# Regions at multiples of 512 bytes, and a planner that issues in a second pass

## The chip, the cores and the metric

One core of a Trainium2 chip runs the whole program in one launch. The metric is the device time of one execution in microseconds; it is compared as the median of several executions, and each text names the run it speaks of. Engines are named as in the profile: PE (TensorE, the matrix unit; PEld are its weight loads), DVE (VectorE), ACT (ScalarE), POOL (GpSimd) and SP (SyncE, which here issues all DMAs).

## The reference

The kernel computes a decoder trunk of two layers over 256 positions with a width of 1024, in float32. Each layer has a feed-forward part, a mixer and a second feed-forward part; a norm ends it:

```python
for l in range(DEPTH):
    x = x + FFN_HALF * swiglu(rms_norm(x, ffn1_norm[l]), ffn1_w_gate_up[l], ffn1_w_down[l])
    u = rms_norm(x, mix_norm[l]) @ w_in[l]
    u_ssd, u_ml, u_rw = jnp.split(u, [D_SSD_IN, D_SSD_IN + D_MLSTM_IN], axis=-1)
    y_ssd = ssd_mixer(u_ssd, ...)      # Mamba-2: convolution, decays, two chunks of 128
    y_ml = mlstm_mixer(u_ml, ...)      # chunked matrix memory with gates
    y_rw = rwkv7_mixer(u_rw, ...)      # a recurrence over time, 8 heads of 64
    y = jnp.concatenate([y_ssd, y_ml, y_rw], axis=-1)
    x = x + y @ w_out[l]
    x = x + FFN_HALF * swiglu(rms_norm(x, ffn2_norm[l]), ffn2_w_gate_up[l], ffn2_w_down[l])
return rms_norm(x, final_norm)
```

The weights are some 200 MB and are read once; the activations are small.

## The kernel before

**The work.** Activations stay on the chip. Each piece of weights (128 x 1024 floats, 512 KB) comes by DMA into a raw buffer. ACT (L784) and DVE (L785) split it into a high and a low half in the PE's fast float format, and three matmuls (L817, L818, L819: high-high, high-low, low-high) make up one product at nearly full precision. In the feed-forward parts L1036, L1038 and L1041 do the like with the activations as the moving side. The mixer's own small products are in plain float32; one such instruction shows as two records of the profile.

**The mixer.** Its combined projection is done in blocks of 128 columns (24 matmuls of 256 columns each, L817 to L819), in a fixed order of groups. A block is evacuated by ACT (L1156, L1155) and DVE (three L1158, a causal convolution) or the like. Meanwhile the three mixers run as soon as their columns are there. In the RWKV part, DVE inverts small triangular blocks in a chain of short instructions (L1327, L1329, L1331), SP writes the result and its transpose to DRAM (`dg`, L1334; `dh`, L1335) and reads them back in another layout (L1343, 16 small DMAs). PE transposes other operands in the meantime (L1351, evacuated by ACT L1353; L1363, whose bank DVE L1366 and ACT L1364 and L1365 read). Then five sets of 64x64 products (L1393, 32 instructions each) complete the inverse, with ACT (L1402, L1411) and DVE (L1406, L1407, L1413) between them; the first needs dg, the second dh. L1439, L1444, L1450, L1453 and L1435 are the recurrence over the four chunks. L1577 and L1578 (evacuated by L1581) make decays; L1599, L1608, L1628, L1654 are the mLSTM; L1720 (transposes, read by DVE L1721 and L1723), L1739 (DVE) and L1751 (PE) are the SSD; L1170 are transposes of finished outputs, which go into the product with `w_out`.

**Buffers.** Nearly all data lie in 22 regions of 2048 floats per partition, each cut into 16 blocks of 128 floats. A region is either of kind `f` (float32) or `r` (the fast format) and may change its kind when it is empty. Behind the constants and one tile `smalls` the regions follow one another in memory, 8192 bytes each.

**What sets the order.** All engine calls are first recorded as operations. A planner, `Planner.run`, then goes through them like a list scheduler: it keeps a model time for each engine, looks at each engine's available operations, takes the one that can start first (by its class and rank among equals), gives its new buffers a place and issues it. `find` looks for the place: raw weights (class `w`) go to the high end of a hole, all else to the low end; the hole that is free soonest and is smallest wins. `may_open` and `keep_max` hold space back. So the queue of every engine is what the planner made of costs and free space, and where a buffer lies decides what can be placed next to it, and when. In this version each operation is issued at the moment it is planned.

Of the kernel before, what the change touches and what calls it, by code (L numbers as in the profile page):

```python
# [64 lines left out]
class Buf:  # L65


    def __init__(self, kind, n, cls):
        self.kind, self.n, self.cls, self.group = kind, n, cls, None
        self.left, self.place, self.where, self.end = 0, None, None, 0.0  # L70
        self.acc = []
        self.pe = None
        self.dests = []
# [79 lines left out]
class Op:  # L153
    __slots__ = ("line", "n", "eng", "call", "name", "a", "k", "bufs", "left", "succ", "ready", "cross", "occ", "dur", "table", "tail",
                 "rank", "piece", "dense", "gate", "lock", "issued", "nbytes", "start", "wait_all")


class Planner:
# [18 lines left out]


    def turn(self, i, kind):
        self.sides[i] = kind  # L180
        self.tiles[i] = self.pool.tile([128, BLOCKS * GRAIN], F32 if kind == "f" else F32R, tag=f"region{i}",
                                       name=f"region{i}")

    def new(self, n, cls="t", kind="f"):
        buf = Buf(kind, n, cls)
        if cls == "t" and kind == "f" and self.group:
            buf.group = self.group
            self.wanted[self.group] = self.wanted.get(self.group, 0) + n
        v = self.tiles[0][:, 0:n]
        return Ref(buf, v if kind == "f" else v.bitcast(F32R))  # L190
# [21 lines left out]
    def add(self, eng, name, call, a, k):  # L212
# [28 lines left out]
        op.left = len(preds)  # L241
# [15 lines left out]
    def touch(self, op, v, write, preds):  # L257
        if isinstance(v, Ref):
            if v.buf not in op.bufs:
                op.bufs.append(v.buf)  # L260
                v.buf.left += 1
            acc = v.buf.acc
            if v.buf.kind == "bank" and op.eng == "pe":

                if v.buf.pe is not None:
                    preds.add(v.buf.pe)
                v.buf.pe = op
        elif v.space == "DRAM" or "dram" in v.tensor.name:
            w = self.dram.setdefault(v.tensor.name, [])
            if write:  # L270
                w.append(op)
            else:
                preds.update(w)
            return
        else:
            acc = self.base.setdefault(v.tensor.name, [])
# [81 lines left out]
    def run(self, reserve, wmin, wmax, urgent, keep_max, spare):  # L358
        ops = self.ops
        for op in reversed(ops):  # L360
            op.tail = op.dur + max((s.tail for s in op.succ), default=0.0)
# [13 lines left out]
        def find(buf, t):  # L375
# [10 lines left out]
            if buf.group:  # L386

                keep = min(keep_max, sum(self.wanted.get((buf.group[0], g), 0) for g in range(buf.group[1])))
# [7 lines left out]
            for i in range(REGIONS):  # L396
                empty = st["free"][i] == BLOCKS
                if st["free"][i] < n or (self.sides[i] != buf.kind or self.tiles[i] is None) and not empty:
                    continue
# [4 lines left out]
                if empty and (self.sides[i] != buf.kind or n == BLOCKS):  # L404
# [18 lines left out]
        def may_open(buf):  # L423

            left = sum(1 for i in range(REGIONS) if st["free"][i] == BLOCKS or self.sides[i] == "r")
            return left > (spare if buf.cls == "w" and st["w"]["f"] >= wmin["f"] else wmin["r"])

        def taken(buf, i):
            buf.where = i
            if buf.kind == "bank":  # L430
                bank_free[i] = INF
                used[buf.cls] += 1
                buf.place = self.banks[i]
            elif buf.kind == "small":
                slot_free[i] = INF
                buf.place = self.smalls[:, i * SLOT:i * SLOT + buf.n]
            else:
                (i, j), n = i, -(-buf.n // GRAIN)
                if self.sides[i] != buf.kind or self.tiles[i] is None:
                    self.turn(i, buf.kind)  # L440
# [4 lines left out]
                buf.place = self.tiles[i][:, j * GRAIN:j * GRAIN + buf.n]  # L445
                if buf.cls == "w":
                    st["w"][buf.kind] += 1
                if buf.group:
                    self.wanted[buf.group] -= buf.n
# [66 lines left out]
        while todo:  # L516
# [18 lines left out]
            assert best is not None, self.stuck(avail, used, grid, st)  # L535
# [3 lines left out]
            for b in places(op):  # L539
# [4 lines left out]
                taken(b, i)  # L544
            if op.lock:
                start = max(start, t)
            if op.table and op.table != st["table"]:
                st["table"] = op.table
                self.nc.scalar.preload_act_table_set(
                    "natural_log_exp_and_others" if op.table == "E" else "silu_and_others")  # L550
# [31 lines left out]
            todo -= 1  # L582

# [7 lines left out]
def kernel(ctx: ExitStack, tc: tile.TileContext, x, pvec, prow, fnorm, w_gate,  # L591
# [27 lines left out]
    smalls = const.tile([128, SLOT * SLOTS], F32, name="smalls")  # L619
# [1308 lines left out]
```

## Time and profile before

| | |
|---|---|
| median of the 3 runs | 1295.01 us (1294.98 to 1297.09) |
| the profiled execution | 1296.8 us |
| its span, first to last instruction | 1294.9 us |
| PE, DVE, ACT, POOL busy | 97%, 69%, 55%, 7% of the span |
| DMA | 210.22 MB, 162 GB/s in the mean |
| mean granted clock of PE | 0.993 |

Times in the profile's rows count from the start of the span. The first feed-forward part lasts to about 199 us, the mixer of layer 0 to about 459, two feed-forward parts to about 840, the mixer of layer 1 to about 1096, the last feed-forward part to the end. A row of idle time names what ended it; PE's ends are modelled, so idle time of PE is a lower bound of what it lost.

### The profile page before, as it was taken

Reading aid. Unit: us, or ns where it says so; the run is one execution under the profiler, and the core shown is the slowest. Engines: PE = TensorE matmul, PEld = TensorE weight load, DVE = VectorE, ACT = ScalarE, POOL = GpSimd, SP = SyncE. Lnnn points to the kernel's source line nnn. Section 1 sums busy time; section 2 is a strip of 40 time slices with the busy share of each in tenths; the row PEclk is TensorE's granted clock in tenths of the full one; section 3 lists DMA queues with packets and bytes.
Section 4 is the critical chain, followed back from the end, with each engine's and each line's share of the span. In section 5 each row is a group of like instructions: output and inputs, shape, how many; then the busy total and the mean of one; then the engine's idle time right before and its main releaser. Section 6 shows DMA issues by size and latency. Waiting matters only on the chain.

```text
span 1294.9 us, 20867 instructions
## 1 busy us (share of the span) xinstructions
PE 1249.7 (97%) x7890; PEld 1077.5 (83%) x7890; DVE 894.7 (69%) x1442; ACT 715.1 (55%) x1241; POOL 90.1 (7%) x161
## 2 busy tenths in 40 slices
PE   7999999987999999999999999999899999999997
PEld 6888887986997878888878888779789888888886
DVE  6766666984699566666676666669837984766664
ACT  7555545664654365555465555565556543655553
POOL 3000002120100010000000000011201010000001
PEclk9999999998999999999999999999999999999999
DMA  9996645152065967765576666530513575976300
GB/s 288 320 292 184 189 129 131 34 124 49 18 220 203 265 185 215 221 187 150 175 217 187 186 193 179 147 82 3 139 34 115 180 257 165 280 208 189 121 1 33
DMA packets 281876, 210.22 MB, mean 162 GB/s; under 512 B 23856, under 2 KB 257200, under 8 KB 281776
## 3 DMA queue, kind: packets, MB, share of 16 engines
q1 hardware_dynamic: 281776, 208.89, 55.4%
q8 instruction: 62, 1.02, 0.3%
q14 instruction: 38, 0.31, 0.1%
HBM read 207.01 MB, written 1.84 MB: 161 GB/s over the span
## 4 chain that ended last, share of the span: by engine, by line
PE 85%; DVE 6%; ACT 3%; DMA 2%; SPq 1%; issue 1%; POOL 0%; POOLq 0%; DVEq 0%; ACTq 0%
PE bank L1036 20%; PE bank L819 13%; PE bank L818 13%; PE bank L817 13%; PE bank L1038 12%; PE bank L1041 3%; PE bank L1393 1%; DVE region L785 1%; PE bank L1751 1%; DMA region<-in_f_gu_dram 1%; DMA region<-dn 1%; ACT region L784 1%; PE bank L1444 1%; PE bank L1453 1%; PE bank L1608 1%
## 5 line engine op out<-in xcount | busy, mean ns | idle before, releaser
L785 DVE TENSOR_TENSOR region<-region,region 128x1024 fp32r<-128x1024 f32 (+1 forms) x382 | 444.4, 1208 | 57.1 <-ACT region L784 52.5
L1036 PE MATMUL bank<-region,region 128*128 128x512 f32 x1120 | 398.2, 398 | 0.0
L817 PE MATMUL bank<-region,region 128*128 128x512 f32 (+1 forms) x1104 | 386.7, 350 | 0.5 <-DVE region L1267 0.4
L818 PE MATMUL bank<-region,region 128*128 128x512 f32 (+1 forms) x1104 | 384.7, 349 | 0.0
L819 PE MATMUL bank<-region,region 128*128 128x512 f32 (+1 forms) x1104 | 384.1, 349 | 0.5 <-DVE region L836 0.5
L784 ACT ACTIVATE region<-region 128x1024 fp32r<-128x1024 f32 (+1 forms) x382 | 376.1, 1038 | 7.6 <-DVE region L1676 2.1
L1038 PE MATMUL bank<-region,region 128*128 128x256 f32 x1280 | 346.5, 281 | 0.0
L1036 PEld LDWEIGHTS bank<-region,region 128*128 128x128 f32 x1120 | 210.4, 188 | 50.9
L1038 PEld LDWEIGHTS bank<-region,region 128*128 128x128 f32 x1280 | 241.6, 189 | 6.5
L819 PEld LDWEIGHTS bank<-region,region 128*128 128x128 f32 x1104 | 210.1, 190 | 27.9 <-DVE region L836 1.5
L818 PEld LDWEIGHTS bank<-region,region 128*128 128x128 f32 x1104 | 210.0, 190 | 25.9 <-issue 0.5
L817 PEld LDWEIGHTS bank<-region,region 128*128 128x128 f32 x1104 | 210.1, 190 | 25.7 <-issue 1.3
L1049 ACT ACTIVATE region<-bank 128x256 f32<-128x256 f32 (+1 forms) x84 | 30.9, 373 | 220.2 <-PE bank L1041 220.2
L1051 DVE TENSOR_TENSOR region<-bank,region 128x256 f32<-128x256 f32 (+1 forms) x84 | 34.2, 410 | 127.0 <-ACT region L1049 127.0
L836 DVE TENSOR_TENSOR region<-region,region 128x256 fp32r<-128x256 f32 (+2 forms) x88 | 36.9, 424 | 35.6 <-ACT region L835 35.6
L1053 ACT ACTIVATE region<-region 128x256 f32<-128x256 f32 (+1 forms) x84 | 34.0, 408 | 49.3 <-DVE region L1052 49.3
L1041 PE MATMUL bank<-region,region 128*128 128x512 f32 x160 | 60.2, 399 | 0.0
L835 ACT ACTIVATE region<-region 128x256 fp32r<-128x256 f32 (+2 forms) x88 | 36.2, 416 | 37.4 <-DVE region L1055 37.0
L853 POOL TENSOR_SCALAR smalls<-smalls 128x1 f32<-128x1 f32 x14 | 6.7, 479 | 616.3 <-ACT region L849 616.0
L849 ACT ACTIVATE region<-res 128x512 f32<-128x512 f32 x28 | 17.6, 629 | 54.0 <-DVE res L845 51.5
L1158 DVE SCALAR_TENSOR_TENSOR region<-bank,pv,region 128x255 f32<-128x255 f32 (+2 forms) x84 | 39.6, 479 | 5.9 <-ACT region L1155 2.9
L1055 DVE TENSOR_TENSOR region<-region 128x256 f32<-128x256 f32 (+1 forms) x76 | 32.0, 422 | 10.9 <-ACT region L1053 2.4
(310 smaller groups left out, 1086.4 us busy)
## 6 DMA issues: line engine op xcount, KB each, us to landing
region<-in_f_gu_dram SPq DMA_DIRECT2D x352, 256.0 KB, 5.4
region<-in_f_dn_dram SPq DMA_DIRECT2D x88, 512.0 KB, 4.8
region<-in_w_in_dram SPq DMA_DIRECT2D x80, 512.0 KB, 4.8
region<-in_w_out_dram SPq DMA_DIRECT2D x32, 512.0 KB, 4.9
region<-in_prow_dram SPq DMA_DIRECT2D x4, 512.0 KB, 5.2
region<-in_prow_dram SPq DMA_DIRECT2D x6, 256.0 KB, 3.7
region<-in_w_gate_dram SPq DMA_DIRECT2D x2, 512.0 KB, 3.6
dn<-region SPq DMA_DIRECT2D x64, 4.0 KB, 1.5
```

The source lines that it names most:

```text
L784: act.activation(out=hi[:, c], in_=src[:, c], func=AF.Copy)
L785: dve.tensor_tensor(out=lo[:, c], in0=src[:, c], in1=hi[:, c].bitcast(F32), op=ALU.subtract)
L817: pe.matmul(o, lhsT=ah, rhs=bh, start=start, stop=False, skip_group_check=True)
L818: pe.matmul(o, lhsT=ah, rhs=bl, start=False, stop=False, skip_group_check=True)
L819: pe.matmul(o, lhsT=al, rhs=bh, start=False, stop=stop, skip_group_check=True)
L835: act.activation(out=hi, in_=src, func=AF.Copy)
L836: dve.tensor_tensor(out=lo, in0=src, in1=hi.bitcast(F32), op=ALU.subtract)
L1036: pe.matmul(o, lhsT=wh[:, k, g, :], rhs=hT.both(kk), start=kk == 0, stop=False, skip_group_check=True)
L1038: pe.matmul(o[:, T:], lhsT=wl[:, k, g, :], rhs=hT(kk)[0], start=False, stop=False, skip_group_check=True)
L1041: pe.matmul(o, lhsT=wh[:, k, g, :], rhs=hT.both(kk), start=False, stop=True, skip_group_check=True)
L1051: dve.tensor_tensor(out=s[:, ts], in0=gate[:, ts], in1=s[:, ts], op=ALU.add)
L1158: dve.scalar_tensor_tensor(out=dst[:, s:T], in0=ps[:, 0:T - s], scalar=col(cw + 3 - s), in1=dst[:, s:T], op0=ALU.mult, op1=ALU.add)
```

## The change

Three things change in the source. The tile `smalls` gets 56 more columns (224 bytes), so region 0 starts at byte 40960 of a partition instead of 40736: 0 instead of 288 past a multiple of 512 bytes, and all regions with it. The planner no longer issues while it plans: `run` only notes for each operation its place in the order, the buffers that it opens and the regions that change their kind, and `emit` issues them afterwards; with that, `run` can be tried with several `keep_max` until one yields a plan. And the list of kinds is kept differently: a region not yet used was of kind `f` before, and has no kind now, except region 0.

```diff
-        self.sides, self.tiles = ["f"] * REGIONS, [None] * REGIONS
+        self.tiles = [None] * REGIONS
         self.turn(0, "f")
+        self.template = self.tiles[0]
...
     def run(self, reserve, wmin, wmax, urgent, keep_max, spare):
+
         ops = self.ops
+        bufs = {b for op in ops for b in op.bufs}
+        for b in bufs:
+            b.left, b.place, b.where, b.end = b.uses, None, None, 0.0
+        wanted = dict(self.wanted)
+        for op in ops:
+            op.left, op.issued, op.ready, op.cross, op.start, op.turns, op.placed = op.npred, False, 0.0, 0.0, None, [], []
+        sides = ["f"] + [None] * (REGIONS - 1)
...
-                if st["free"][i] < n or (self.sides[i] != buf.kind or self.tiles[i] is None) and not empty:
+                if st["free"][i] < n or sides[i] != buf.kind and not empty:
                     continue
...
-                if empty and (self.sides[i] != buf.kind or n == BLOCKS):
+                if empty and (sides[i] != buf.kind or n == BLOCKS):
                     fits.append((max(float(blocks.max()), t), BLOCKS, i, 0))
                     continue
...
-                buf.place = self.tiles[i][:, j * GRAIN:j * GRAIN + buf.n]
+                buf.place = True
...
-            assert best is not None, self.stuck(avail, used, grid, st)
+            if best is None:
+                self.jam = self.stuck(avail, used, grid, st)
+                return False
...
-            call_from(op.line, op.call, [v.at() if isinstance(v, Ref) else v for v in op.a],
-                      {n: v.at() if isinstance(v, Ref) else v for n, v in op.k.items()})
-            op.issued = True
+            op.issued = len(log)
...
+    def emit(self):
+
+        for op in sorted(self.ops, key=lambda op: op.issued):
...
+            for b in op.placed:
...
+                    b.place = self.tiles[i[0]][:, i[1] * GRAIN:i[1] * GRAIN + b.n]
+            call_from(op.line, op.call, [v.at() if isinstance(v, Ref) else v for v in op.a],
+                      {n: v.at() if isinstance(v, Ref) else v for n, v in op.k.items()})
...
-    smalls = const.tile([128, SLOT * SLOTS], F32, name="smalls")
+    smalls = const.tile([128, SLOT * SLOTS + 56], F32, name="smalls")
...
+    assert any(plan.run(reserve={"f": 6144, "r": 6144}, wmin={"f": 4, "r": 4}, wmax={"f": 5, "r": 6},
+                        urgent={"act": 7000.0, "dve": 5500.0}, keep_max=keep, spare=8)
+               for keep in (3072, 4096, 6144, 8192)), plan.jam
     with tc.manual_schedule():
-        plan.run(reserve={"f": 6144, "r": 6144}, wmin={"f": 4, "r": 4}, wmax={"f": 5, "r": 6}, urgent={"act": 7000.0, "dve": 5500.0}, keep_max=3072, spare=8)
+        plan.emit()
```

The last of the three changes `find`: an `f` buffer that opens an unused region now falls under `sides[i] != buf.kind` and is put at block 0, where a raw weight was put at the region's high end before. From there on free space lies otherwise, and the plan differs from some point on. The lines of the mixer stand 30 lines further down in the new source (L1363 is L1393 there, L1393 is L1423, L817 is L847).

The engines get the same instructions in the same numbers. PE's order is the same up to the second group of L1363 in layer 0. Before, at the place where PE waits for dg and dh, its queue has the rest of a block (weights in `region_2317`), transposes, and then the 64x64 products (L1393):

```order
L817 MATMUL bank_88<-region_628,region_2317 128x256
L818 MATMUL bank_88<-region_628,region_2317 128x256
L819 MATMUL bank_88<-region_628,region_2317 128x256
L1351 MATMUL bank_90<-ident,region_1811 128x128 x4
L1351 MATMUL bank_91<-ident,region_1811 128x128 x4
L1439 MATMUL bank_89<-region_2520,region_2178 64x64 x4
L1439 MATMUL bank_89<-region_2520,region_347 64x64 x4
L1351 MATMUL bank_88<-ident,region_1811 128x128 x4
L1363 MATMUL bank_90<-ident,region_1859 128x128 x4
L1351 MATMUL bank_91<-ident,region_1811 128x128 x4
L1393 MATMUL bank_88<-region_827,region_584 64x64 x4
```

Now PE takes the second L1363 (L1393 in the new source) at once and goes on with a new block (weights in `region_672`):

```order
L848 MATMUL bank_88<-region_175,region_2319 128x256
L849 MATMUL bank_88<-region_175,region_2319 128x256
L1393 MATMUL bank_90<-ident,region_1860 128x128 x4
L847 MATMUL bank_91<-region_628,region_672 128x256
L848 MATMUL bank_91<-region_628,region_672 128x256
L849 MATMUL bank_91<-region_628,region_672 128x256
```

and the first 64x64 products (now L1423) come behind the last matmul of that block, two of the next, a group of transposes and a first L1599 (now L1629):

```order
L849 MATMUL bank_91<-region_175,region_672 128x256
L847 MATMUL bank_89<-region_628,region_2061 128x256
L848 MATMUL bank_89<-region_628,region_2061 128x256
L1381 MATMUL bank_90<-ident,region_911 128x128 x4
L1629 MATMUL bank_92<-region_696,region_1841 128x128
L1423 MATMUL bank_93<-region_846,region_1704 64x64 x4
```

In all, 26 projection matmuls moved ahead of the first 64x64 product, and 15 between these products. On ACT, which evacuates the banks at the same place, the order before is:

```order
L1365 ACTIVATE region_2623<-bank_89 64x512
L1353 ACTIVATE region_942<-bank_90 128x512
L1353 ACTIVATE region_892<-bank_91 128x512
L1581 ACTIVATE region_2520<-bank_92,region_892 128x128
L1441 ACTIVATE region_2674<-bank_89 64x512
L1353 ACTIVATE region_2674<-bank_88 128x512
L1364 ACTIVATE region_2623<-bank_90 64x512
```

and now (L1364 is L1394, L1365 is L1395, L1581 is L1611, L1441 is L1471, L1353 is L1383, L1156 is L1186, L1402 is L1432):

```order
L1395 ACTIVATE region_2625<-bank_89 64x512
L1394 ACTIVATE region_2625<-bank_90 64x512
L1395 ACTIVATE region_1040<-bank_90 64x512
L1611 ACTIVATE region_2522<-bank_92,region_1841 128x128
L1611 ACTIVATE region_2522<-bank_93,region_1841 128x128
L1611 ACTIVATE region_2522<-bank_87,region_1841 128x128
L1471 ACTIVATE region_1841<-bank_88 64x512
L1383 ACTIVATE region_2665<-bank_89 128x512
```

The second L1364 and L1365 moved ahead of the evacuations of L1351. SP's queue there is the same: dg, dh, eight and eight DMAs back.

More of the change, by code (lines that the diff above doesn't have):

```diff
@@ L69, in __init__ @@
         self.kind, self.n, self.cls, self.group = kind, n, cls, None
-        self.left, self.place, self.where, self.end = 0, None, None, 0.0
+        self.left, self.place, self.where, self.end, self.uses = 0, None, None, 0.0, 0
         self.acc = []
@@ L154 @@
     __slots__ = ("line", "n", "eng", "call", "name", "a", "k", "bufs", "left", "succ", "ready", "cross", "occ", "dur", "table", "tail",
-                 "rank", "piece", "dense", "gate", "lock", "issued", "nbytes", "start", "wait_all")
+                 "rank", "piece", "dense", "gate", "lock", "issued", "nbytes", "start", "wait_all", "npred", "turns", "placed")
 class Planner:
@@ L188, in new @@
             self.wanted[self.group] = self.wanted.get(self.group, 0) + n
-        v = self.tiles[0][:, 0:n]
+        v = self.template[:, 0:n]
         return Ref(buf, v if kind == "f" else v.bitcast(F32R))
@@ L240, in add @@
                 v.buf.dests += [b for b in op.bufs if b.kind in "fr" and b not in v.buf.dests]
-        op.left = len(preds)
+        op.npred = len(preds)
         for p in preds:
@@ L260, in touch @@
                 op.bufs.append(v.buf)
-                v.buf.left += 1
+                v.buf.uses += 1
             acc = v.buf.acc
@@ L386, in find @@
             if buf.group:
-                keep = min(keep_max, sum(self.wanted.get((buf.group[0], g), 0) for g in range(buf.group[1])))
+                keep = min(keep_max, sum(wanted.get((buf.group[0], g), 0) for g in range(buf.group[1])))
                 if (st["room"] - n) * GRAIN < keep:
@@ L423, in may_open, with taken @@
         def may_open(buf):
-            left = sum(1 for i in range(REGIONS) if st["free"][i] == BLOCKS or self.sides[i] == "r")
+            left = sum(1 for i in range(REGIONS) if st["free"][i] == BLOCKS or sides[i] == "r")
             return left > (spare if buf.cls == "w" and st["w"]["f"] >= wmin["f"] else wmin["r"])
-        def taken(buf, i):
+        def taken(op, buf, i):
             buf.where = i
+            op.placed.append(buf)
             if buf.kind == "bank":
@@ L432, in taken @@
                 used[buf.cls] += 1
-                buf.place = self.banks[i]
+                buf.place = True
             elif buf.kind == "small":
                 slot_free[i] = INF
-                buf.place = self.smalls[:, i * SLOT:i * SLOT + buf.n]
+                buf.place = True
             else:
                 (i, j), n = i, -(-buf.n // GRAIN)
-                if self.sides[i] != buf.kind or self.tiles[i] is None:
-                    self.turn(i, buf.kind)
+                if sides[i] != buf.kind:
+                    sides[i] = buf.kind
+                    op.turns.append((i, buf.kind))
                 grid[i, j:j + n] = INF
@@ L444, in taken @@
                 st["ver"] += 1
-                buf.place = self.tiles[i][:, j * GRAIN:j * GRAIN + buf.n]
+                buf.place = True
                 if buf.cls == "w":
@@ L448, in taken @@
                 if buf.group:
-                    self.wanted[buf.group] -= buf.n
+                    wanted[buf.group] -= buf.n
         def released(buf):
@@ L582, in run @@
             todo -= 1
+        return True
+    def emit(self):
+        for op in sorted(self.ops, key=lambda op: op.issued):
+            for turn in op.turns:
+                if isinstance(turn, str):
+                    self.nc.scalar.preload_act_table_set(
+                        "natural_log_exp_and_others" if turn == "E" else "silu_and_others")
+                else:
+                    self.turn(*turn)
+            for b in op.placed:
+                i = b.where
+                if b.kind == "bank":
+                    b.place = self.banks[i]
+                elif b.kind == "small":
+                    b.place = self.smalls[:, i * SLOT:i * SLOT + b.n]
+                else:
+                    b.place = self.tiles[i[0]][:, i[1] * GRAIN:i[1] * GRAIN + b.n]
+            call_from(op.line, op.call, [v.at() if isinstance(v, Ref) else v for v in op.a],
+                      {n: v.at() if isinstance(v, Ref) else v for n, v in op.k.items()})
     def stuck(self, avail, used, grid, st):
```

6 lines of the change are left out of this document (2 added, 4 removed).

## The prediction

> **What bounds the kernel now.** I read four views, from the whole to the place: the page, the waits of TensorE, the timeline around the longest of them, and the stretches behind it.
>
> ```profile
> span 1294.9 us, 20867 instructions
> PE 1249.7 (97%) x7890; PEld 1077.5 (83%) x7890; DVE 894.7 (69%) x1442; ACT 715.1 (55%) x1241; POOL 90.1 (7%) x161
> PE 85%; DVE 6%; ACT 3%; DMA 2%; SPq 1%; issue 1%; POOL 0%; POOLq 0%; DVEq 0%; ACTq 0%
> q1 hardware_dynamic: 281776, 208.89, 55.4%
> ```
>
> TensorE is busy for 1249.7 of 1294.9 us, so whatever is done to the rest can win at most the 45.2 us in which it stands still. DMA is 2% of the chain that ended last. The waits of TensorE over the whole run (us in total, times, longest) say where those 45 us lie:
>
> ```profile
> PE bank L1363 <- DVE region L1567: 8.6, 2, 6.6
> PE bank L885 <- DMA res<-in_x_dram: 6.2, 2, 4.3
> PE bank L1393 <- DMA region<-dh: 2.2, 1, 2.2
> PE bank L1393 <- DMA region<-dg: 1.2, 1, 1.2
> ```
>
> The first, third and fourth row belong to one place in the mixer of layer 0. There DVE has solved small triangular systems, SP sends the result through DRAM (dg, dh) and back, and the 64x64 products of L1393 wait for it. The timeline there, first TensorE, then SP, DVE and ACT (start, length, in brackets the idle time before and what ended it):
>
> ```profile
> 287.11 0.28 PE L818 MATMUL bank<-region,region 128*128 128x256 f32 x1
> ...
> 289.27 0.28 PE L818 MATMUL bank<-region,region 128*128 128x256 f32 x1
> 296.17 1.08 PE L1363 MATMUL bank<-ident,region 128*128 128x128 f32 x4 [6.63 <-DVE region L1567]
> ...
> 300.04 1.17 PE L1439 MATMUL bank<-region,region 128*64 128x64 f32 x16 [0.22 <-issue]
> ...
> 303.83 2.38 PE L1393 MATMUL bank<-region,region 64*64 64x64 f32 x64 [1.15 <-DMA region<-dg]
> 308.41 6.01 PE L1393 MATMUL bank<-region,region 64*64 64x64 f32 x192 [2.20 <-DMA region<-dh]
> 314.81 2.08 PE L1393 MATMUL bank<-region,region 64*64 64x64 f32 x64 [0.39 <-ACT region L1411]
> 316.82 1.56 PE L1608 MATMUL bank<-region,region 128*128 128x256 f32 x6
> 321.99 0.61 PE L1599 MATMUL bank<-region,region 128*128 128x128 f32 x4
> 322.43 1.06 PE L1450 MATMUL bank<-region,region 128*128 128x128 f32 x8
> ```
>
> ```profile
> 296.96 3.85 SPq L1343 DMA_DIRECT2D region<-dg  x8
> 300.91 5.26 SPq L1343 DMA_DIRECT2D region<-dh  x8
> ...
> 302.35 0.69 DVE L1366 TENSOR_TENSOR region<-bank,smalls 128x512 f32<-128x512 f32 x1 [1.47 <-PE bank L1351]
> ...
> 303.07 0.59 ACT L1364 ACTIVATE region<-bank 64x512 f32<-64x512 f32 x1 [0.52 <-DVE region L1366]
> ```
>
> So behind the 6.63 us come four more stops: 0.22 + 1.15 + 2.20 + 0.39 = 3.96 us. In all of them TensorE has projection work that it could do but that stands later in its queue. Behind this place the changed stretch of layer 0, and all of the changed stretch of layer 1, have none:
>
> ```profile
> 323.70:356.10 32.40, 32.40 (x322) 30.71 (x321) 19.70 (x45) 21.82 (x46) 5.22 (x6) 1.00 0.06 18
> 356.10:388.50 32.40, 32.40 (x266) 30.91 (x267) 30.19 (x51) 19.10 (x28) 2.67 (x2) 1.00 0.69 220
> 388.50:420.80 32.30, 32.30 (x166) 24.95 (x165) 29.72 (x38) 15.20 (x25) 2.87 (x4) 1.00 0.56 203
> 1003.50:1035.90 32.40, 32.40 (x203) 28.03 (x203) 31.20 (x46) 18.44 (x25) 2.75 (x2) 1.00 0.55 180
> ```
>
> (Columns: stretch, its length, then busy us and instructions of PE, PEld, DVE, ACT, POOL, the granted clock, the DMA share and GB/s.) TensorE fills each stretch; DVE comes close to it in three of the four.
>
> **The change, part by part.** It says that it moves addresses. The order says that it also moves instructions, so there are three parts.
>
> *Addresses.* The pad puts the regions from 288 bytes past a multiple of 512 to 0. If an engine cared, tiles that lie elsewhere would read or write at another pace already: `res` lies 384 past, `br` and `selr` 160 and 128 past.
>
> ```profile
> L849 ACT ACTIVATE region<-res 128x512 f32<-128x512 f32 x28 | 17.6, 629 | 54.0 <-DVE res L845 51.5 <-DMA res<-in_x_dram 2.1
> L1767 ACT ACTIVATE region<-region 128x512 f32<-128x512 f32 x8 | 5.0, 626 | 15.1 <-DVE region L1766 15.1
> L845 DVE SCALAR_TENSOR_TENSOR res<-bank,smalls,res 128x512 f32<-128x512 f32 x16 | 11.4, 745 | 8.3 <-PE bank L819 7.5 <-POOL region L951 0.9
> L1770 DVE SCALAR_TENSOR_TENSOR region<-region,smalls,region 128x512 f32<-128x512 f32 x8 | 5.6, 744 | 0.6 <-POOL smalls L831 0.6
> L1577 PEld LDWEIGHTS bank<-br,selr 128*128 128x128 f32 x40 | 6.0, 189 | 0.2
> L1038 PEld LDWEIGHTS bank<-region,region 128*128 128x128 f32 x1280 | 241.6, 189 | 6.5
> ```
>
> 629 against 626, 745 against 744, 189 against 189 ns: I cost the addresses at 0 for ACT, DVE and TensorE. No tile here lies at 0 past 512, so a gain at exactly that place is not excluded; the rows nearest to it say none. For the transfers nothing in the trace separates the old address from another one. The bound comes from who waits: TensorE's three DMA rows above are 6.2 + 2.2 + 1.2 = 9.6 us, of which the 6.2 us are for `res`, which does not move. A transfer would have to become a fifth shorter to show even 2 us. I take 0, with bounds from -2 us (a fifth of 9.6) to +2 us.
>
> The Trainium skill, "DMA: Bandwidth & Descriptors", section "How a descriptor splits into AXI transactions", says that a descriptor which does not start at a multiple of 256 bytes fetches from the boundary below it, and pays for the bytes ahead of its start. It tells this of reads, and here the regions are mostly written; for a run of 512 bytes that starts 32 past the boundary it would be 17 beats of 32 bytes instead of 16, by my estimate from that page 6%. The sum would then be lower by 6% of 9.6 us, 0.6 us. No row here shows it.
>
> *Two passes.* The plan is made first and issued afterwards; the instructions that TensorE, DVE, ACT, POOL and SP get are the same in number and kind (the built orders differ in place alone), and the first of the four values of `keep_max`, the old 3072, already yields a plan. What it costs on the chip: 0, since planning is done before there is a program.
>
> *The order.* Because unopened regions now count as neither kind, the first raw weights go to the low end of their region and the free space falls otherwise. From the second group of transposes of L1363 on, the plan of layer 0 differs, that of layer 1 from 991 us of the old run on (the first L1170 that stands elsewhere). Ahead of that, and with it the wait of 6.63 us and all of the start, nothing is moved. At the place above 41 matmuls of the projections (L817 to L819, 256 columns) come ahead: 15 + 1 + 10 behind the second L1363 and before the first L1393, 1 + 14 between the L1393; so do the eight matmuls of L1599. Their prices: from 287.11 to 289.27 are 18 matmuls, so 0.12 us each, 41 x 0.12 = 4.9 us; L1599 takes (322.43 - 321.99) / 4 = 0.11 us a record and makes two records an instruction, 16 x 0.11 = 1.8 us. Together 6.7 us of work, more than the 3.96 us of holes. SP's row of dg and dh transfers stands where it stood, so dh still lands at about 308.4.
>
> I follow the new queue of TensorE with those rows. It has the second L1363 at about 298.8, the 15 matmuls until 301.3 (the clock is half until about 300, as before), L1439 until 302.4, the transposes L1351 with 11 matmuls between them until 305.9. The dg products thus start two us later than at 303.83, when dg has long landed: the 0.22 and 1.15 are gone. ACT is what is late next. It now has L1364 directly behind L1365, and this waits for DVE's second L1366, which stands behind three instructions of L1158, until about 301.6, and ACT idles for some 1.6 us in which it evacuated L1351 before; so the bank that the second half of the dg products needs is read out at about 306.6, 0.4 us after TensorE wants it. The dg products end at 308.7, when dh is there: the 2.20 us is gone. The rest of L1599 follows (until 310.3), the next 96 products (6.0 us, until 316.4), 14 matmuls (1.7 us, which cover L1411 and its 0.39 us) and the last 32 (2.1 us): 320.2 us, where the old kernel stands at 316.8. It is 3.4 us later there with 6.7 us more done. Gain 3.3 to 3.4 us; I take 3.4.
>
> *What lies behind.* The 41 matmuls are missing as cover later. In layer 0, between the transposes L1720 and the products L1751 there are now 10 projection matmuls instead of 14, and DVE's work on them must be done meanwhile. DVE is the tight engine there (29.72 and 30.19 of 32.4). It is helped by the same move, since splits of weights (L785) that stood there now stand ahead of 335 us, where it idles. I cost it at 0, cover being what is left of the projections; the bounds are 0 and the rival below. In layer 1 nothing waits in the changed part, so nothing can be won and I take 0 there too, bounds 0 and +2 us (a wait as long as dh's above).
>
> **The sum.** -3.4 us on the profiled execution's 1296.8 us (span 1294.9 and 1.9 around it) gives 1293.4. That execution lies 1.8 us above the median of the runs, 1295.01, so I forecast the median at 1291.6. About 0.2%, 2.6 us, is what a measurement of this kernel can tell from no change.
>
> **Rivals.**
> - *Given back.* The place gains as worked out, but one or two small waits of the size of dg's and dh's rows (1.2 to 2.2 us) appear behind it, in layer 0 where DVE is tight or in layer 1. For it: DVE at 92% and 96% of two stretches. Against: the old plan had the same load there and no wait of TensorE. Time: 1291.6 + 1.2 to 1291.6 + 3.4, about 1294.
> - *DVE becomes the bound in layer 0's tail (slower).* Place: the first L1751 behind L1720. There DVE has in a row three L1739, an L1723, an L1730, a fourth L1739 and a split L785. If DVE is behind by this whole row when TensorE arrives, it costs 4 x 1.22 + 2 x 0.69 + 1.22 = 7.5 us, from the rows below, less the 3.4 us won: 1299.1. It decides from a lag of 6 us on.
>
> ```profile
> L1739 DVE TENSOR_TENSOR region<-region,region 128x1024 f32<-128x1024 f32 x7 | 8.4, 1219 | 0.0
> L1723 DVE TENSOR_TENSOR region<-bank,region 128x512 f32<-128x512 f32 x8 | 5.5, 688 | 1.6 <-PE bank L1720 1.3 <-issue 0.2
> L785 DVE TENSOR_TENSOR region<-region,region 128x1024 fp32r<-128x1024 f32 x374 | 439.3, 1220 | 56.6 <-ACT region L784 52.0 <-DMA region<-in_w_in_dram 2.6 <-DMA region<-in_f_gu_dram 1.6
> ```
>
> - *The addresses do what they are changed for.* Transfers get shorter by up to a fifth, and the waits for dg, dh and the first weights with them: 2 us more, 1289.6. The rule above would make 0.6 us of it. For it speaks nothing in the trace, against it that TensorE waits 9.6 us for DMA in all, of which 6.2 are not moved and 3.4 are already won.
> - *The order is not what counts, and the addresses do nothing:* the filled work only moves a wait to behind 308 us. Against it stands that dh lands at 308.4 either way, with all else landed. 1295.
>
> **How the numbers follow.** Gain as summed, nothing given back: 0.47, own range 1290 to 1292.4. More than that through transfers or a wait in layer 1 that goes too: 0.13, down to 1287.5. Given back, or no effect: 0.27, 1292.4 to 1297.6. DVE's rival or another new wait of its kind: 0.13. Faster by over 0.2% is under 1292.4: 0.60; within: 0.27; slower: 0.13. The range, which leaves out the ends of the second and most of the last case, is 1288 to 1297.
>
> **What would show it.** In the changed profile the wait of 6.6 us ahead of the first L1363 (now L1393) is still there; the waits of the 64x64 products (now L1423) for dg and dh are under 0.5 us together; projections stand between 298 and 306 us; the last of the 64x64 products ends near 320 us. TensorE's LDWEIGHTS, ACT's and DVE's mean durations are unchanged to 1%; so is the start up to the first projection of layer 0. It is wrong if TensorE shows new waits for DVE or ACT between 330 and 460 us or 985 and 1095 us that add up to over 1 us, or if matmuls of one kind start at another distance than before.

## The result and the profile after

The changed kernel takes 1289.2 us (median; 1287.96 to 1291.69), against 1295.9 us for the kernel before on the same chip: a ratio of 0.9947, 95% interval 0.9933 to 0.9962, some 6.7 us. The forecast was 1291.6 us with a range of 1288 to 1297, which holds the measured time; but its gain, 3.4 us, is half of the measured one. The profiled execution took 1288.72 us. Its page, in the lines that answer to those shown of before (span; busy time of the engines; shares of the chain that ended last; the transfer queue):

```profile
span 1286.6 us, 20888 instructions
PE 1251.0 (97%) x7890; PEld 1079.2 (84%) x7890; DVE 896.0 (70%) x1442; ACT 715.9 (56%) x1241; POOL 91.9 (7%) x161
PE 88%; DVE 6%; ACT 4%; DMA 1%; issue 1%; POOL 0%; POOLq 0%; SPq 0%; DVEq 0%; ACTq 0%
q1 hardware_dynamic: 281776, 208.89, 53.5%
```

The engines do what they did before. TensorE is busy 1.3 us longer and stands still for 35.6 us of the span where it was 45.2, 9.6 us less. The queue moves the same 208.89 MB, but its packets took 53.5% of the 16 engines' span and not 55.4%. TensorE's waits after (us in total, times, longest):

```profile
PE bank L1393 <- DVE region L1597: 6.4, 2, 4.4
PE bank L1423 <- ACT region L1432: 0.9, 1, 0.9
PE bank L1423 <- ACT region L1441: 0.4, 1, 0.4
```

The wait ahead of the first transposes (L1363, now L1393) is 4.4 us and not 6.6. Its row names L1597 (before, L1567), a short DVE instruction that stands in DVE's queue behind the whole solve of the small triangular systems: before, the solve starts at 287.39 us and L1567 at 296.02. So in what follows this wait is called the wait for the solve. The waits of the 64x64 products (L1393, now L1423) for dg and dh are gone; the two rows that are left, for ACT, lie in layer 1. The place in layer 0, first TensorE and then SP:

```profile
291.34 1.09 PE L1393 MATMUL bank<-ident,region 128*128 128x128 f32 x4 [4.42 <-DVE region L1597]
...
301.80 2.13 PE L1423 MATMUL bank<-region,region 64*64 64x64 f32 x64
303.86 1.83 PE L1629 MATMUL bank<-region,region 128*128 128x128 f32 x14
305.73 5.86 PE L1423 MATMUL bank<-region,region 64*64 64x64 f32 x192
313.39 2.13 PE L1423 MATMUL bank<-region,region 64*64 64x64 f32 x64
315.45 2.42 PE L1638 MATMUL bank<-region,region 128*128 128x256 f32 x10
```

```profile
292.13 4.83 SPq L1373 DMA_DIRECT2D region<-dg  x8
297.06 3.83 SPq L1373 DMA_DIRECT2D region<-dh  x8
```

No row of the 64x64 products has a bracket any more: nothing stops them. They end at 315.45 us, 1.4 us ahead of the old 316.82, with some 6.7 us more work done (by the prediction's prices). But TensorE also comes to this place sooner: its first transposes start at 291.34 us and not at 296.17. Of these 4.8 us, 2.6 lie ahead of the wait (its last projection starts at 286.64 us, before at 289.27), and two later profiles of the changed kernel don't repeat most of it (289.67 and 288.75). The other 2.2 us are the shorter wait. They were won before the first instruction that the change moves, in the round trip of dn through DRAM that feeds the triangular solve (L1327, now L1357). Before, SP and then DVE:

```profile
275.94 0.90 SPq L1301 DMA_DIRECT2D dn<-region  x2
276.94 3.72 SPq L709 DMA_DIRECT2D region<-in_w_in_dram  x4
280.85 2.17 SPq L1304 DMA_DIRECT2D region<-dn  x1
```

```profile
287.39 0.19 DVE L1327 TENSOR_TENSOR region<-region,region 128x15 f32<-128x15 f32 x1 [2.81 <-DMA region<-dn]
```

After:

```profile
273.01 0.89 SPq L1331 DMA_DIRECT2D dn<-region  x2
274.00 3.66 SPq L739 DMA_DIRECT2D region<-in_w_in_dram  x4
277.89 1.26 SPq L1334 DMA_DIRECT2D region<-dn  x1
```

```profile
282.54 0.19 DVE L1357 TENSOR_TENSOR region<-region,region 128x15 f32<-128x15 f32 x1 [0.29 <-DMA region<-dn]
```

Between the writes of dn and its read SP issues four loads of weights, 2 MB. They fill the gap in which the writes land, but the read lies behind them in the transfer queue. From the first of these loads to the start of the solve it was 10.45 us (276.94 to 287.39) and is now 8.54 (274.00 to 282.54). DVE waited 2.81 us for dn and waits 0.29; TensorE's wait for the solve is 2.2 us shorter. The old page showed the read of dn in its chain that ended last, though not as a wait of TensorE; from issue to landing it took 6.52 us there in layer 0 and 4.83 in layer 1:

```profile
PE bank L1036 20%; PE bank L819 13%; PE bank L818 13%; PE bank L817 13%; PE bank L1038 12%; PE bank L1041 3%; PE bank L1393 1%; DVE region L785 1%; PE bank L1751 1%; DMA region<-in_f_gu_dram 1%; DMA region<-dn 1%; ACT region L784 1%; PE bank L1444 1%; PE bank L1453 1%; PE bank L1608 1%
```

### The profile page after: what moved, and what is told of

Read it like the earlier page. It is cut to its first block, busy times and chain, and to the rows that moved or that the text cites. A ratio compares the mean times of both kernels' runs of the same rounds, so it can differ in the third digit from the quotient of the medians.

```text
span 1286.6 us, 20888 instructions
## 1 busy us (share of the span) xinstructions
PE 1251.0 (97%) x7890; PEld 1079.2 (84%) x7890; DVE 896.0 (70%) x1442; ACT 715.9 (56%) x1241; POOL 91.9 (7%) x161
## 3 DMA queue, kind: packets, MB, share of 16 engines
q1 hardware_dynamic: 281776, 208.89, 53.5%
## 4 chain that ended last, share of the span: by engine, by line
PE 88%; DVE 6%; ACT 4%; DMA 1%; issue 1%; POOL 0%; POOLq 0%; SPq 0%; DVEq 0%; ACTq 0%
PE bank L1066 20%; PE bank L847 14%; PE bank L849 14%; PE bank L848 14%; PE bank L1068 12%; PE bank L1071 3%; PE bank L1423 1%; PE bank L1781 1%; DVE region L815 1%; ACT region L814 1%; PE bank L1483 1%; PE bank L1474 1%; ACT region L919 1%; PE bank L915 1%; PE bank L1638 1%
## 5 line engine op out<-in xcount | busy, mean ns | idle before, releaser
L815 DVE TENSOR_TENSOR region<-region,region 128x1024 fp32r<-128x1024 f32 (+1 forms) x382 | 444.5, 1209 | 56.7 <-ACT region L814 55.7
L1066 PE MATMUL bank<-region,region 128*128 128x512 f32 x1120 | 398.1, 398 | 0.0
L847 PE MATMUL bank<-region,region 128*128 128x512 f32 (+1 forms) x1104 | 387.6, 351 | 0.5 <-DVE region L1297 0.4
L1066 PEld LDWEIGHTS bank<-region,region 128*128 128x128 f32 x1120 | 210.4, 188 | 50.9
L847 PEld LDWEIGHTS bank<-region,region 128*128 128x128 f32 x1104 | 211.2, 191 | 25.0 <-DVE region L1297 0.8
L866 DVE TENSOR_TENSOR region<-region,region 128x256 fp32r<-128x256 f32 (+2 forms) x88 | 36.9, 424 | 35.6 <-ACT region L865 35.6
L865 ACT ACTIVATE region<-bank 128x512 fp32r<-128x512 f32 x28 | 16.7, 598 | 42.5 <-PE bank L1200 21.5
```

The lines of the kernel that those rows point to most:

```text
L815: dve.tensor_tensor(out=lo[:, c], in0=src[:, c], in1=hi[:, c].bitcast(F32), op=ALU.subtract)
L847: pe.matmul(o, lhsT=ah, rhs=bh, start=start, stop=False, skip_group_check=True)
L865: act.activation(out=hi, in_=src, func=AF.Copy)
L866: dve.tensor_tensor(out=lo, in0=src, in1=hi.bitcast(F32), op=ALU.subtract)
L1066: pe.matmul(o, lhsT=wh[:, k, g, :], rhs=hT.both(kk), start=kk == 0, stop=False, skip_group_check=True)
```

## The experiments

Theory: order and addresses act separately. The order fills the holes of dg and dh; the addresses make transfers faster, and what TensorE sees of it is the solve that starts sooner, because dn's read lies behind weights. Rivals: the order is all, and the rest is chance; or faster transfers help everywhere. "Before" is run beside each group of kernels: 1295.94 us beside the first four (the addresses alone, the order alone, 320 past, the changed kernel again), 1297.2 beside the next, 1295.78 beside the last three.

### The addresses alone

The kernel before, with the pad of the change:

```diff
-    smalls = const.tile([128, SLOT * SLOTS], F32, name="smalls")
+    smalls = const.tile([128, SLOT * SLOTS + 56], F32, name="smalls")
```

> The old order with all regions at multiples of 512 bytes (the pad alone). If the addresses carry half of the gain, 3 to 4 us: about 1292 where the kernel before has 1295.5; the fifth product of the first layer starts near 6.8 us instead of 7.8, the wait for the solved triangles (first L1363) is about 4.4 us instead of 6.6, and the 64x64 products still wait for dg and dh (3.4 us together, or less where the transfers land sooner). If the order is all and the earlier start is chance: 1295.5 within 2 us, with the waits of the kernel before.

1293.4 us, ratio 0.9981 (0.9971 to 0.999): 2.5 us faster, with an interval of 1.3 to 3.8. Its waits and its start of the solve, every instruction standing where it stood before:

```profile
PE bank L1363 <- DVE region L1567: 7.1, 2, 5.1
```

```profile
285.06 0.19 DVE L1327 TENSOR_TENSOR region<-region,region 128x15 f32<-128x15 f32 x1 [1.35 <-DMA region<-dn]
293.86 1.09 PE L1363 MATMUL bank<-ident,region 128*128 128x128 f32 x4 [5.10 <-DVE region L1567]
```

DVE's wait falls from 2.81 to 1.35 us and TensorE's from 6.63 to 5.10, each by 1.5. So the addresses do act, and here. They act at the 64x64 products, too, where the waits for dg (1.15 us) and dh (2.20 us) were expected to remain:

```profile
302.50 1.90 PE L1393 MATMUL bank<-region,region 64*64 64x64 f32 x56 [0.93 <-ACT region L1365]
304.90 4.60 PE L1393 MATMUL bank<-region,region 64*64 64x64 f32 x140 [0.51 <-ACT region L1402]
310.05 1.73 PE L1393 MATMUL bank<-region,region 64*64 64x64 f32 x52 [0.55 <-issue]
312.19 2.08 PE L1393 MATMUL bank<-region,region 64*64 64x64 f32 x64 [0.41 <-ACT region L1411]
```

No row names dg or dh any more; shorter waits, mostly for ACT, have taken their place, and the idle time between 300 and 400 us falls from 3.7 to 2.5 us. This is one profile. Another expectation missed: the fifth product of the first layer starts at 7.95 us, no sooner than before.

### The order alone

The changed kernel without the pad.

> The new order with the regions where they were, 288 bytes past a multiple of 512. If order and addresses both count: 3.3 us faster than before, about 1292, with a wait of about 6.6 us ahead of the first L1393, no waits for dg and dh, and the start as before (fifth product near 7.8 us). If the order is all: about 1289, with the wait at 4.4 us. If the filled holes are paid back somewhere: 1295.

1291.98 us, ratio 0.9966 (0.9955 to 0.9976): 4.0 us faster (3.1 to 5.8). The wait for the solve is nearly what it was (6.28 us for 6.63), and behind it no row of TensorE up to 322 us has a wait:

```profile
295.61 1.09 PE L1393 MATMUL bank<-ident,region 128*128 128x128 f32 x4 [6.28 <-DVE region L1597]
...
316.93 2.13 PE L1423 MATMUL bank<-region,region 64*64 64x64 f32 x64
```

In the same group the changed kernel was run again. Expected were about 1289 us, a fifth product near 6.8 us, a wait of 4.4 us for the solve, and stretches at half clock elsewhere than at the 833, 857 and 929 us of its first profile. It took 1290.34 us, ratio 0.995 (0.9933 to 0.9967). The wait is 4.1 us; the fifth product starts at 7.92 us, and two of the stretches stand at 857 and 929 us again, so these two expectations missed.

The two parts come to 2.5 + 4.0 = 6.5 us, where both together gave 6.7 at first and 5.6 in this group. On top of the order the addresses are thus worth 1.6 us and not 2.5. That fits with the dg and dh holes, in which both win and which can be won only once, but the difference is within the noise.

### Which address counts

The changed kernel with other pads: 8 floats put the regions at 320 past a multiple of 512, 120 floats at 256 past. Each got its own run:

> The new order with the regions 320 bytes past a multiple of 512: at a multiple of 64, but not of 128, 256 or 512. If what costs is a start that is no multiple of 64: as the changed kernel, about 1289. If a multiple of 256 or 512 is needed: as the new order at the old addresses, about 1292. If addresses do nothing, both and this are the same.

> The new order with the regions 256 bytes past a multiple of 512. If a start at a multiple of 256 is enough: nearly all 512-byte packets take 27 ns, as with the regions at 0, and the time is that of the changed kernel, about 1290. If a multiple of 512 is needed: a third of the packets take 28 to 41 ns, as at 288 and at 320, and the time is that of the new order alone, about 1292.

At 320: 1291.15 us, ratio 0.9961 (0.9945 to 0.9977); at 256: 1289.64 us, ratio 0.9941 (0.9929 to 0.9953). The first interval overlaps that of the order alone and that of the changed kernel; the time doesn't decide it. The durations of the single packets in the traces show which addresses make packets slow. Worked out over all 224256 packets of 512 bytes of each run:

```
regions past 512   kernel              over 27 ns   mean ns
288                before                35.2%       30.3
288                order alone           32.8%       30.1
320                new order             28.8%       29.9
256                new order              1.3%       28.2
0                  addresses alone        1.4%       28.3
0                  changed kernel         1.3%       28.1
```

The median is 27 ns everywhere; off a multiple of 256 some 28 to 34% of the packets take 28 to 41 ns, on one hardly any. For fast packets a multiple of 64 isn't enough and a multiple of 512 isn't needed.

### The transfers by themselves

This kernel leaves out the whole computation and was executed once; only stretches of its one profile are compared, with one another.

```diff
+    for p, (kind, off, busy) in enumerate(PLAN):
+        v = big[:, off // 4:off // 4 + 6144].rearrange("p (s c) -> p s c", s=6)
+        for s in range(6):
...
+                nc.sync.dma_start(out=raw.rearrange("p (k c) -> p k c", k=8),
+                                  in_=w_in[0][:, n * 128:n * 128 + 128].rearrange("(k p) c -> p k c", p=128))
...
+        nc.vector.tensor_copy(out=sm[:, p], in_=v[:, :, 512])
```

> Leaves the whole computation out: only weight transfers of 512 KB, six at a time into one tile, whose start goes through 0, 32, 64, 128, 256, 288 and 320 bytes past a multiple of 512, with runs of 512, 1024 and 4096 bytes; at the end the same with VectorE and ScalarE at work beside them. If the address by itself makes a packet slow: runs of 512 bytes take 27 ns at 0 and 256, and up to 35 ns in the mean at 32 and 288, and six transfers take up to 10% longer. If it does so only beside engines that use the memory: a difference only in the phases with engines at work. If the difference between the two kernels is one of their plans: none anywhere.

Eight windows of 8 us, one inside each stretch of six loads with runs of 512 bytes, at 0, 32, 64, 128, 256, 288, 320 and again 0 bytes past 512 (busy us and instructions of DVE, ACT and POOL, clock, DMA share, GB/s):

```profile
14.00:22.00 8.00, 7.76 (x8) 7.78 (x8) 0.00 (x0) 1.00 1.15 346
27.00:35.00 8.00, 7.79 (x7) 7.78 (x8) 0.00 (x0) 1.00 1.16 295
40.00:48.00 8.00, 7.79 (x7) 7.78 (x8) 0.00 (x0) 1.00 1.17 297
53.00:61.00 8.00, 7.76 (x8) 5.29 (x6) 0.00 (x0) 1.00 1.19 299
66.00:74.00 8.00, 7.76 (x8) 0.00 (x0) 0.00 (x0) 1.00 1.15 347
78.00:86.00 8.00, 0.00 (x0) 0.00 (x0) 0.00 (x0) 1.00 1.16 299
92.00:100.00 8.00, 0.00 (x0) 0.00 (x0) 0.00 (x0) 1.00 1.17 296
105.00:113.00 8.00, 0.00 (x0) 0.00 (x0) 0.00 (x0) 1.00 1.15 346
```

346 GB/s at 0 and 256, 295 to 299 at every other address: 14 to 15% less. VectorE's and ScalarE's work, which depends on nothing, ran in the first windows and not at the end; 346 stands beside busy and beside idle engines, so they aren't the cause. With runs of 1024 bytes the windows show 366 to 371 GB/s at 0 and 256 and 340 to 357 elsewhere, with runs of 4096 bytes 404 to 408 and 392 to 397: the loss shrinks as the runs get longer.

The Trainium skill, "DMA: Bandwidth & Descriptors", section "How a descriptor splits into AXI transactions", has the boundary of 256 bytes that shows here. The estimate from it in the prediction, 17 beats for 16 or 6%, is too small against these windows. By the same estimate a start at 128 (20 beats) would also cost more than one at 32 (17 beats): 299 and 295 GB/s don't show that.

### dn ahead of the weights, in the old order

If dn is late because it lies behind weights, reading it first should give what the addresses give, and more. The old order and old addresses, with only SP's queue changed; what SP issues between the last write of dn (1348 there) and its read (1351) is put behind the read:

```diff
+        for pm in [o for o in order if o.eng == "sp" and o.line == 1351]:
...
+            for o in reversed(order[:p]):
+                if o.eng == "sp":
+                    if o.line == 1348:
+                        break
+                    held.insert(0, o)
...
+                order.insert(p, order.pop(q))
```

> The kernel before (old order, old addresses), in which one thing moves on SP's queue: the read of dn is issued ahead of the 2 MB and 1.75 MB of weights that stood between it and the writes of dn. If the addresses help there only because dn lies behind the weights in the transfer queue: DVE's waits of 2.81 and 1.15 us for dn vanish, TensorE's 6.6 us ahead of the first L1363 become about 3.8, and the kernel is 3 to 4 us faster, about 1292, with packets as slow as before. If dn is late for another reason (its own small packets, the writes ahead of it): the waits stay and the time is 1296. If the weights, now later, are missed: slower than 1296.

1305.97 us, ratio 1.0066 (1.0051 to 1.0081): 8.8 us slower. TensorE's longest wait for the solve falls to 3.1 us and dn is waited for no more, but the weights are missed (ACT and DVE in layer 0, then TensorE's new wait over both layers; L831 and L832 are L784 and L785, L1625 is L1578):

```profile
288.10 1.06 ACT L831 ACTIVATE region<-region 128x1024 fp32r<-128x1024 f32 x1 [7.56 <-DMA region<-in_w_in_dram]
```

```profile
289.19 1.23 DVE L832 TENSOR_TENSOR region<-region,region 128x1024 fp32r<-128x1024 f32 x1 [7.40 <-ACT region L831]
```

```profile
PE bank L1625 <- ACT region L1628: 12.4, 2, 7.0
```

A split of weights stands in ACT's and DVE's queues ahead of everything else, and the solve stands behind it on DVE. In the old plan these weights came just in time: DVE's split of them starts at 281.94 us after a wait of 0.15 us. The mechanism of dn wasn't refuted by this, but the edit put something else in its place.

### dn ahead of the weights, planned

The same rule, given to the planner instead, in the changed kernel:

```diff
-            if op.gate > st["prog"]:
+            if op.gate > st["prog"] or op.eng == "sp" and st["hold"] and op.line != 1337:
                 return False
...
+            if op.line in (1334, 1337):
+                st["dn"] += op.line == 1334
+                st["hold"] = op.line == 1334 and st["dn"] % 32 == 0
```

(1334 writes dn, 1337 reads it.) It was run twice, the second time beside the changed kernel and beside the same plan with the regions back at 288 past 512.

> The changed kernel, with a planner that issues nothing on SP between the last write of dn and its read, and plans everything with that. If the wait of 4.4 us in layer 0 can be won by an earlier dn: DVE starts its triangular solve up to 5 us sooner, and the kernel is 2 to 5 us faster than the changed one, 1285 to 1288. If the new plan only puts other work late (weights, splits on DVE): 1290 or more, with new waits of TensorE between 300 and 460 us.

> The plan with dn's read directly behind its writes, regions at multiples of 512, once more: 9 to 11 us below the kernel before, about 1286.5, if the first measurement holds; its second profile shows which of the waits of the first recur.

> The changed kernel on the same chip as these two: 6 to 7 us below the kernel before, so that the plan with dn first is 3 us better, or the same if the difference between the two was one of chips.

> The plan in which nothing stands between dn's writes and its read, with the regions back at 288 bytes past a multiple of 512. If the addresses win their 2 to 2.5 us mainly because dn lies behind weights in the transfer queue, little of it is left here: within 1 us of the same plan at multiples of 512 (about 1287). If slower transfers cost by themselves, everywhere: the full 2 to 2.5 us more, about 1289.

1286.53 us (ratio 0.9915, 0.9901 to 0.993) and 1284.27 us (0.9914, 0.9901 to 0.9926); the changed kernel beside the second 1290.01 us (0.9952, 0.9938 to 0.9965). This plan beats both kernels, the changed one by 5.7 us on that chip. In the second profile DVE starts the solve at 281.61 with no wait, TensorE's longest wait for it is 1.7 us, and the price is a small wait for weights of L1599 (L1632):

```profile
PE bank L1396 <- DVE region L1600: 2.9, 2, 1.7
PE bank L1632 <- DMA region<-in_wv_dram: 2.3, 2, 1.3
```

```profile
277.69 0.34 SPq L1337 DMA_DIRECT2D region<-dn  x1
```

```profile
281.61 0.18 DVE L1360 TENSOR_TENSOR region<-region 128x15 f32<-128x15 f32 x1
```

With the regions at the old addresses this plan takes 1285.23 us (0.9916, 0.9902 to 0.9929), though 31.9% of its 512-byte packets take over 27 ns. The addresses are worth 1.0 us here, with the two sets of times overlapping, and 2.5 us where dn lies behind the weights; from the times alone these two can't be told apart. TensorE's idle time tells more: with this plan it is 26.7 us at the old addresses and 27.2 at the new ones, with the old order 37.7 and 34.3. DVE starts the solve without a wait at both. So slow packets cost little by themselves in this kernel; they cost where something late stands behind many of them.

### All profiles in one table

TensorE's idle time (gaps over 30 ns between its records, counted where a gap begins), in us, by stretch of the run:

```
kernel                    all   0-100  200-300  300-400  900-1000
before                   37.7     6.9     10.5      3.7       8.2
addresses alone          34.3     7.1      8.9      2.5       7.6
order alone              32.6     6.7     10.0      0.0       7.2
order, 320 past          31.4     6.7      9.8      0.0       7.0
order, 256 past          30.2     7.1      8.5      0.0       5.9
changed, first           28.1     6.0      8.3      0.0       5.6
changed, second          30.8     7.0      8.7      0.0       6.5
changed, third           28.9     6.7      8.0      0.0       6.1
dn first, planned        28.6     6.6      7.7      0.1       5.6
dn first, planned again  27.2     6.6      7.0      0.1       4.7
same, old addresses      26.7     6.7      6.8      0.1       4.6
dn first, queue alone    44.8     7.4     13.3      4.7      12.2
```

The order empties the stretch 300 to 400, of which the addresses alone take 1.2 us. The stretch 200 to 300 follows the addresses (8.0 to 8.9 on a multiple of 256, 9.8 to 10.5 off it, with the old plan of SP). Between 900 and 1000, the same place in layer 1, it is less with either; but TensorE's order there is as before up to 991 us, so that order doesn't explain the 1.0 us less of the order alone, and its cause stays open. The start follows neither: its 6.0 in the first profile after didn't recur in the next two (7.0 and 6.7). Of the planned version's lead of 5.7 us over the changed kernel only 1.4 us are idle time (27.9 in the mean of two profiles against 29.3 of three). Another 2.9 us are TensorE's busy time (1248.3 against 1251.2 us in these profiles). It goes with the stretches in which TensorE's granted clock is 0.50: they add up to 17.3 us against 23.0, and half of that difference is 2.9 us. Whether the plan or chance makes them fewer stays open.

The clock can be taken out roughly. Time and mean granted clock are on record for 102 executions of the whole kernels. A straight line through them, with one constant for each kernel and group, gives 0.54 us of time for each us of clock lost. At equal clock, by this estimate, the addresses alone are worth 1.9 us (1.2 to 2.5), the order alone 4.1 (3.3 to 4.8) and the changed kernel beside them 5.8 (4.9 to 6.7); in the last group the planned version leads the changed kernel by 4.3 us (3.1 to 5.4), and its two addresses are 0.0 us apart (within 1.1). Part of the lost clock may itself be a kernel's doing, so these figures are rough.

## Why the prediction was right, and where not

**The order: right.** The step said that 41 projection matmuls fill the holes of dg and dh, 3.4 us. The order alone measured 4.0 us (3.1 to 5.8), and the idle time of that stretch fell from 3.7 us to 0. The last of the 64x64 products ends at 319.1 us there, where the step followed them to 320.2. The 0.4 us taken off because ACT would be late with a bank didn't occur. For the changed part of layer 1 the step took 0, and the idle time from 1000 us on is 0.8 us before and with the order alone.

**What lies behind: right.** No new wait of TensorE appeared between 330 and 460 us: its idle time from 400 to 500 us is 0.8 before and 0.7 after, and from 1000 us on 0.8 in both. Neither the given-back rival nor DVE's came true.

**The engines' indifference to addresses: right.** The chain's largest groups have the same mean duration before and after (L1036, now L1066: 398 and 398 ns; L785, now L815: 1208 and 1209).

**The addresses' term, 0 us: mis-sized; it measured 2.5 us (1.3 to 3.8) in the old order and 1.6 us on top of the new one.** Two sentences failed. "For the transfers nothing in the trace separates the old address from another one" holds for the rows that were read, which group the transfers; the single packets of the same trace had a spread that was not looked at, 35.2% of them over their median of 27 ns. And the bound "who waits: TensorE's three DMA rows" left out the largest wait of all. The row L1363 <- DVE, 8.6 us, names the engine that released TensorE; that engine had itself waited 2.81 and 1.15 us for dn. A bound on a resource has to follow the waits back through the engine between. The sentence that this wait would still be 6.6 us, since nothing moves ahead of it, falls with it: 4.4 us, and 4.1 and 4.5 in the two later profiles. The prediction put the whole row into layer 0; 2.0 of its 8.6 us lie in layer 1, and there they stay 2.0 although DVE's wait for dn goes from 1.15 us to nothing.

**The third rival,** transfers shorter by up to a fifth and 2 us from them, came nearest: 14 to 15% less rate for runs of 512 bytes, 2.5 us of time. It had been given a small chance because TensorE's DMA waits were few. It named dg, dh and the first weights as the places; the runs show the round trip of dn, which it didn't name, and dg and dh, which the order fills anyway. So it is partly luck that its 1289.6 us stands beside 1289.2 measured. The forecast's 1291.6 is the order's part alone, which measured 1291.98; the range held because it left room for other gains, not because the addresses were foreseen.

**The start: right in the end.** The first profile after seemed to contradict "the start unchanged" (fifth product at 6.84 us, before 7.81); the second and third have it at 7.92 and 7.62.

## What to carry to other kernels

A wait for an engine can be a wait for a transfer one step back: before a resource is called harmless, look at what the releasing engine itself waited for, and what stands ahead of that in the queue. A small transfer that a chain needs soon should not be issued behind megabytes of prefetch, but moving it in the queue alone can make the prefetch late; let the plan of the other engines move with it. Start tiles that receive runs of 512 bytes at a multiple of 256 bytes: here that was worth 14 to 15% of the transfer rate.

## What was not expected of the hardware

The address changes a transfer in a step and not by degrees: at 32, 64, 128, 288 and 320 bytes past a multiple of 512 the rate is the same 295 to 299 GB/s, at 0 and 256 it is 346 or 347. In the kernel most packets at a bad address are still fast (before, 65% at 27 ns or less); in the loads by themselves only 22 to 30% are at the bad addresses.

TensorE's clock halves in stretches of 3.4 or 6.8 us, and once more at the very end of a run. Many of them come and go between executions, but not just anywhere: the three profiles of the changed kernel each have one near 292, one near 858 and one near 930 us, two of them have one near 834, and two one between 200 and 223. Before, and in the new order at 256 past (columns as in the prediction):

```profile
201.20:204.60 3.40, 3.24 (x9) 2.21 (x8) 3.40 (x5) 0.16 (x1) 0.63 (x2) 0.50 0.59 154
```

```profile
201.20:204.60 3.40, 3.40 (x19) 2.79 (x19) 2.79 (x4) 0.31 (x1) 0.00 (x0) 1.00 0.00 0
```

In both a wait of 1.67 us lies just ahead; in the first the clock then falls to 0.50 and TensorE gets 9 matmuls done, in the second it stays and it gets 19 done. Over a whole execution of the kernels in the table these stretches, the last one included, add up to between 11.2 us (planned again) and 37.5 us (queue alone), and three profiles of the changed kernel had 22.3, 20.5 and 26.2. So two single profiles can differ by a few us without a cause in the code, and a difference of 2 us is read from several executions or from idle time.
